# Nine of eleven row pairs of an FFN's last projection as block products, with every second weight's low parts on GpSimd

## The chip, the cores and the metric

The kernel runs on one core of a Trainium2 chip. The metric is the device time of one execution in microseconds (us), and the kernel before has a median of 843.04 us over three runs (843.0 to 843.1). A core has engines that run side by side, each with its own queue of instructions: TensorE (PE, with its weight loads shown as PEld), VectorE (DVE), ScalarE (ACT), GpSimd (POOL) and SyncE (SP). In this kernel SP issues most of the DMA transfers, and POOL issues a few that add while they copy.

## The reference, cut to what matters

One residual block on 512 tokens of width 1024, all in float32: a mixing part (attention over chunks, and a gated recurrence), and then a SwiGLU feed-forward network, which is what this case is about.

```python
hn = rmsnorm(h, norm_ffn_g[l])
gu = hn @ w_ffn_in[l]                  # 1024 x 5632
g, up = jnp.split(gu, 2, axis=-1)      # 512 x 2816 each
h = h + (jax.nn.silu(g) * up) @ w_ffn_out[l]   # 2816 x 1024
return rmsnorm(h, final_norm_g)
```

The last projection multiplies the activations (512 x 2816) by `w_ffn_out` (2816 x 1024). With tiles of 128, the 2816 rows of the weight are 22 row tiles, or 11 pairs of them.

## The kernel before, in words

**Float32 out of two parts.** TensorE works here on a reduced float32 format. Each operand is split into a high part, which ACT makes by a copy, and a low part, the rest, which DVE makes by a subtraction (`split`, lines 84 to 87). A product is then three matmuls (`mm3`, lines 78 to 82: lines 80, 81 and 82 of the profile): high by high, high by low, low by high. The first reads only high parts; the second is the first to read the weight's low part.

**Block products.** A row pair with its two row tiles, and the tokens and output columns in halves, is a 2 x 2 by 2 x 2 product of blocks. Done plainly it takes eight block products, 48 matmuls of 512 columns. It can be had from seven block products, 42 matmuls, if sums and differences of blocks are multiplied instead. The kernel does three pairs plainly (`plain`, pairs 0 to 2) and eight as block products (`paired`, pairs 3 to 10; `N_PLAIN` on line 34).

For a paired row pair the weight side needs the blocks of the left output half as they are (`fo0`), one block with its sum (`t3b`), and sums of blocks (`t12` and `t4`). These sums are made in DRAM, long before: during the attention SP copies blocks (`out_copy`, `COPIES`), and later POOL issues transfers that add to them (`out_add`, `ADDS_AT`, `ADDS`), one transfer for each group of `GROUP` row pairs. The activation side needs for each pair a left tile (`a_first`), a right tile with four additions on DVE (`a_sums`, lines 1518 to 1526), then a second form of the left tile (`a_second`), and a last part of the right tile (`a_last`). Each ends in a `split`, so in an ACT copy and a DVE subtraction.

**The order of the last projection.** It is written out by hand for PE, DVE and ACT (`manual_schedule`), so these three do their instructions in the order of the code. SP and POOL are put in order by a planner. The stages are:

1. the plain pairs on the left output half (24 matmuls each). After each but the first, left and right tiles are made for the paired ones;
2. P: for each pair two products with `fo0` (`p_one`, `p_two`; 12 matmuls). The second products of the last three pairs are held back to the end. `p_then` spreads the left tiles and some of the right tiles between them;
3. the plain pairs but the last two on the right output half (one pair here, 24 matmuls);
4. T: two products for each pair with `t12` (`t_one`, `t_two`), again with three held back. The remaining right tiles are made one per step, ahead of the weights of that step, and from the fifth pair on the second form of a left tile behind each step;
5. U: two products for each pair with `t3b`. All but the last six pairs come first, with all their first products ahead of their second ones, and then the last six in the same way;
6. the products with `t4`, then the last two plain pairs, the additions to `h`, the norm and the output.

**Weights.** `weights(name, ahead)` makes sure that a weight and `ahead` more after it are on their way, in one fixed list (`fo0`, the right half of the plain pairs but two, `t12`, `t3b`, `t4`, the last two plain ones). Making one means a tile to hold its two parts (seven in turn), a raw tile to load it to (five in turn, free again when the low part is made), the loads on SP, the high part on ACT, and the low part. For `t12`, `t3b` and `t4` the low part is put off (`high_first`, `lows`): it enters DVE's order when the next weight is made (`low_parts`), and so behind whatever the code has put there meanwhile. In T's last step `weights` is asked for `t3b` of the second pair, and only after the left tiles that remain for all the others.

The running sums of the products live in PSUM banks; when a sum is complete DVE adds it to `h` (`h_add`, line 1546; `h_sum`, line 1551). Those additions wait for PE, and what is written behind them on DVE waits too.

Of the kernel before, what the change touches and what calls it, by code (L numbers as in the profile page):

```python
# [9 lines left out]
F32R = mybir.dt.float32r  # L10
# [4 lines left out]
P = 128  # L15
# [15 lines left out]
V_CW, V_CB, V_BR, V_BI, V_LAM, V_BM, V_GF = 0, 32, 40, 48, 56, 64, 80  # L31
NV = 88
CW = 256
N_PLAIN = 3
GROUP = 2
COPIES = [1] * 16
ADDS_AT = (9, 11, 13, 15)
ADDS = {"fg1": 1, "fg2": 1}
PAIR_TILES = 2 * (11 - N_PLAIN) - (4 - (N_PLAIN - 1))


@with_exitstack
def block_kernel(ctx: ExitStack, tc: tile.TileContext, x, norm_mix_g, w_in, b_merge, rel_table,
# [3 lines left out]
    pe, dve, act, pool, sp = nc.tensor, nc.vector, nc.scalar, nc.gpsimd, nc.sync  # L47

    def pool_of(name, bufs=1, side="left"):
        return tc.tile_pool(name=name, bufs=bufs, side=side, reuse_waits="tile")  # L50
# [21 lines left out]
    def f(ap):  # L72
        return ap.bitcast(F32)
# [62 lines left out]

    plain, paired = list(range(N_PLAIN)), list(range(N_PLAIN, FT // 2))

# [44 lines left out]
    def out_raw_home(name):  # L183
        n = raw_count[0] = raw_count[0] + (out_room[0] is not None)
        pl, bufs = (out_room[0], 2) if n % 5 in (2, 4) else (wp, 3)
        return pl.tile([P, 2, S], F32, tag="raw", bufs=bufs, name=f"raw_{name}")

    def out_home(name):
        n = out_count[0] = out_count[0] + 1
        pl, bufs = (wp, 4) if n % 7 in (1, 2, 3, 4) else (out_room[0], 3)  # L190
        return pl.tile([P, 2, 2, S], F32R, tag="whl", bufs=bufs, name=f"whl_{name}")

    lows = []

    def high_first(hi, lo, src):

        act.activation(hi, src, AF.Copy)
        lows.append(lambda: dve.tensor_sub(lo, src, f(hi)))

    def low_parts(n=0):  # L200

        while len(lows) > n:
            lows.pop(0)()

    t4_raw = {}
    groups = [paired[n:n + GROUP] for n in range(0, len(paired), GROUP)]
    out_t = {}
# [6 lines left out]
    def out_t_at(kind, i):  # L214
        t, n = out_t[kind, i]
        return t[:, n]
# [21 lines left out]
    def step(todo, n=1, **more):  # L238

        for _ in range(min(n, len(todo))):  # L240
            what, *of = todo.pop(0)
            what(*of, **more)

    def out_sums(name, rows):

        kind, i = name.split("_")
        i = int(i)
        if kind == "t4":

            hl = spare[0].tile([P, 2, S], F32R, tag="act", bufs=13, name=f"whl_{name}")  # L250
        else:
            hl = out_home(name)

        if kind == "t4":
            if i not in t4_raw:
                raw = out_raw_home(name)
                for n, i_ in enumerate(paired[i - paired[0]:][:2]):
                    sp.dma_start(out=raw[:, n], in_=out_t_at("t4", i_))
                    t4_raw[i_] = raw[:, n]
            raw = t4_raw[i]  # L260
        else:
            raw = out_raw_home(name)
        if kind == "t12":
            sp.dma_start(out=raw[:, 0], in_=out_t_at("t1", i))
            sp.dma_start(out=raw[:, 1], in_=out_t_at("t2", i))
        elif kind == "t3b":
            sp.dma_start(out=raw[:, 0], in_=out_t_at("t3", i))
            sp.dma_start(out=raw[:, 1], in_=w_ffn_out[rows + P:rows + 2 * P, S:])
        else:
            low_parts()  # L270
            high_first(hl[:, 0], hl[:, 1], raw)
            return lambda part, k, at=every: hl[:, part, at]
        low_parts()
        high_first(hl[:, 0], hl[:, 1], raw[:])
        return lambda part, k, at=every: hl[:, part, k, at]

    v_t1, v_t2 = [], []
# [143 lines left out]
    def prefetch(n):  # L421
        while len(made) < min(n, len(chunks), index.get(barrier[0], len(chunks))):
            name, parts, rows, kts = chunks[len(made)]
            if name[:2] == "v_":
                made.append(v_weights(name[2:]))
                continue
            if name[:2] == "o_" or name[:3] == f_units[0]:
                made.append(kept_weights(name[0], name.split("_")[1]))
                continue
            if name[:3] in f_units:  # L430
                made.append(f_weights(*name.split("_")))
                continue
            if not parts:
                made.append(out_sums(name, rows))
                continue
            tiles = []
            wide = sum(width for *_, width in parts)
            step = 4 * CW // wide
            for k in range(0, kts, step):
                n_ = min(step, kts - k)  # L440
                if name in extra:
                    hl = extra[name].tile([P, 2, n_, wide], F32R, tag="whl", bufs=4, name=f"whl_{name}_{k}")
                elif name[:2] == "fo":
                    hl = out_home(name)
                else:
                    hl = wp.tile([P, 2, n_, wide], F32R, tag="whl", bufs=4, name=f"whl_{name}_{k}")
                if (name, k) not in raws:
                    load(name, k)
                raw = raws.pop((name, k))
                low_parts()  # L450
                split(hl[:, 0], hl[:, 1], raw[:])
                tiles.append(hl)
            made.append(lambda part, k, at, tiles=tiles, step=step: tiles[k // step][:, part, k % step, at])

    def weights(name, ahead=1):
        prefetch(index[name] + 1 + ahead)
        if index[name] + 1 == len(made):
            low_parts()
        return made[index[name]]
# [511 lines left out]
    def x_sums():  # L971

        s, s3 = (zp.tile([P, 4, 256], F32, tag="late", bufs=2, name=f"v_s{n}")[:] for n in (1, 3))
        out = {}

        def parted(key, src):
            pl, tag = (aw, "v") if key == "s4" else (aw2, "pt")
            hi, lo = (pl.tile([P, 4, 256], F32R, tag=tag, bufs=4, name=f"v_{key}{n}") for n in "hl")
            split(hi[:], lo[:], src)
            out[key] = hi, lo  # L980

        def chain(dst, first_, *rest):
            (op, one, two) = first_
            tc.keep_in_program_order(op(dst, one, two))
            for op, one in rest:
                op(dst, dst, one)

        add, sub = dve.tensor_add, dve.tensor_sub
        chain(s, (add, x_block(1, 0, 0), x_block(1, 1, 0)), (add, x_block(1, 0, 1)), (add, x_block(1, 1, 1)))
        parted("s1", s)  # L990
        chain(s, (sub, s, x_block(0, 0, 0)), (sub, x_block(0, 0, 1)))
        parted("s2", s)
        chain(s3, (sub, x_block(0, 0, 0), x_block(1, 0, 0)), (add, x_block(0, 0, 1)), (sub, x_block(1, 0, 1)))
        chain(s, (sub, x_block(0, 1, 0), s), (add, x_block(0, 1, 1)))
        return out, parted, s, s3
# [159 lines left out]
    sums = x_sums()  # L1155
# [9 lines left out]
    with tc.manual_schedule(engines={mybir.EngineType.PE}):  # L1165
        v_all(sums)
        for h in range(HEADS):
# [4 lines left out]
            weigh(h, pp)  # L1172
            step(copies, COPIES[h])
            if h in ADDS_AT:
# [11 lines left out]
    for j in range(KT):  # L1186
# [11 lines left out]
        else:  # L1198
            i = j - 4
# [91 lines left out]
    acp = ctx.enter_context(pool_of("act", 13))  # L1291
# [160 lines left out]
    for unit in f_units[1:]:  # L1452
        n, last = int(unit[2]), unit == f_units[-1]
# [51 lines left out]
    left, right_ = {}, {}  # L1505
    spare_tags = ["t10", "t11", "t20", "t21"][N_PLAIN - 1:]
    ohp = []

    def pair_tile(i, name):
        if spare_tags:  # L1510
            return sums_room.tile([P, 2, 2, 256], F32R, tag=spare_tags.pop(), bufs=1, name=f"{name}{i}")
        return ohp[0].tile([P, 2, 2, 256], F32R, tag="act", bufs=PAIR_TILES, name=f"{name}{i}")

    def a_first(i):
# [42 lines left out]
    def h_scale(cc, t, at=every):  # L1557

        if t not in scaled:
            scaled[t] = ohp[0].tile([P, D], F32, tag="act", bufs=PAIR_TILES, name=f"hg{t}")  # L1560
        n = slice(cc * S + at.start, cc * S + at.stop)
# [24 lines left out]
    def spread(todo, n):  # L1586

        for _ in range(min(n, len(todo))):
            todo.pop(0)()

    with tc.manual_schedule(engines={mybir.EngineType.PE, mybir.EngineType.DVE, mybir.EngineType.Activation}):
# [3 lines left out]
        sums = [lambda i=i: a_sums(i) for i in paired]  # L1595
# [34 lines left out]
        pw = {}  # L1630

        def p_one(n, i):
            pw[i] = weights(f"fo0_{i}", 4 if n < 4 else 2)
            if n == 0:
                for t in (2, 3):
                    h_add(0, t, po[t][:])
            for a in range(2):
                out_block(pq[a][:], left[i], 0, a, pw[i], 0, n == 0)
            if i == paired[-1]:
                for a in range(2):  # L1640
                    h_add(0, a, pq[a][:])
# [4 lines left out]

        def p_then(n):
            spread(firsts, 1)
            if n in (1, 3, 5):
                spread(sums, 1)  # L1650

        two_sided(p_one, p_two, p_then)
        for a in range(2):
# [112 lines left out]
```

## Time and profile before

| | |
|---|---|
| median of three runs | 843.04 us |
| the profiled execution | 843.44 us |
| its span, first to last instruction | 841.7 us |
| PE busy | 833.2 us, 99% |
| DVE, ACT, POOL busy | 662.8, 516.7, 160.5 us |
| granted TensorE clock | 0.999 |
| first matmul of the last projection, last one | 726.62, 835.48 us |

Rows of the timeline give the start, the length, the engine, the line of the kernel, the operation, and the tiles (written <- read) with their shapes. "x2" means two instructions of one kind behind each other, whose length is then that of both. Brackets tell how long the engine had been idle before, and what ended it. Instructions that follow each other on DVE overlap a little, so what one costs in a queue is the distance from its start to the next one's.

### The profile page before, as it was taken

The page shows a single profiled execution, that of the slowest core. Times are in us where ns is not written, and L with a number is a line of the kernel's source. Part 1 is how long each engine was busy: PE and PEld are TensorE (multiplying, and loading weights), DVE is VectorE, ACT ScalarE, POOL GpSimd, SP SyncE. Part 2 cuts the span into 40 slices and gives each one's busy share as a digit, 9 for nine tenths or more (in the row PEclk, how much of TensorE's full clock was granted, in tenths as well). Part 3 has the DMA queues.
Part 4 walks back from the last instruction along what each step waited for, and adds up shares of the span by engine and source line. Part 5 has one row for each costly group of instructions (what it writes and reads, how often), then busy time and mean ns, then how long its engine had stood idle before and what let it go on. Part 6 is the DMA issues. An engine that isn't in the chain of part 4 may idle for free.

```text
span 841.7 us, 11921 instructions
## 1 busy us (share of the span) xinstructions
PE 833.2 (99%) x4230; PEld 706.8 (84%) x4230; DVE 662.8 (79%) x974; ACT 516.7 (61%) x850; POOL 160.5 (19%) x219
## 2 busy tenths in 40 slices
PE   8999999999999999999999999999999999999997
PEld 6988888888888888888888888888888999988886
DVE  6688778887959888887568767888777878997784
ACT  7686858774356688878544547663764465455543
POOL 3502030221020043433211012005102321300000
PEclk9999999999999999999999999999999999999999
DMA  8466487553645455538558875555955576644442
GB/s 291 165 228 225 147 300 254 184 206 104 197 156 150 138 149 139 175 129 216 101 136 220 325 280 172 156 176 170 236 170 155 150 189 185 213 154 149 156 171 100
DMA packets 107323, 153.98 MB, mean 183 GB/s; under 512 B 8216, under 2 KB 66160, under 8 KB 106752
## 3 DMA queue, kind: packets, MB, share of 16 engines
q1 hardware_dynamic: 102304, 141.32, 51.6%
q0 software_dynamic: 3728, 8.96, 6.4%
q10 hardware_dynamic: 1232, 2.95, 0.9%
q8 instruction: 33, 0.54, 0.2%
q14 instruction: 26, 0.21, 0.1%
HBM read 139.53 MB, written 30.45 MB: 202 GB/s over the span
## 4 chain that ended last, share of the span: by engine, by line
PE 96%; DMA 2%; DVE 1%; ACT 1%; issue 0%; ACTq 0%; SPq 0%; DVEq 0%
PE fu_x L81 2%; PE fu_x L80 2%; PE fu_x L82 2%; PE o L1134 2%; PE fg_x L80 2%; PE fg_x L82 2%; PE fg_x L81 2%; PE pT L1114 2%; PE s L1085 2%; PE po_xr L80 2%; PE po_xr L81 2%; PE po_gb L80 2%; PE po_ga L80 2%; PE po_gr L82 2%; PE po_xr L82 2%; PE po_gr L80 2%
## 5 line engine op out<-in xcount | busy, mean ns | idle before, releaser
L1098 ACT ACTIVATE p<-p,m 128x384 f32<-128x384 f32 (+2 forms) x64 | 35.8, 559 | 14.9 <-DVE m L1097 14.4
L1103 POOL TENSOR_SCALAR p<-p,rl 128x128 f32<-128x128 f32 (+3 forms) x61 | 37.3, 628 | 14.7 <-DVE rl L1099 13.3
L1355 POOL TENSOR_TENSOR sg<-sg,keep_fu_x 128x512 f32<-128x512 f32 x8 | 14.5, 1817 | 100.3 <-DVE keep_fu_x L1354 100.3
L87 DVE TENSOR_TENSOR pp<-pT,pp 128x384 fp32r<-128x384 f32 (+1 forms) x48 | 27.0, 598 | 4.4 <-ACT pp L86 3.3
L87 DVE TENSOR_TENSOR whl_fu_w<-raw_fu_w,whl_fu_w 128x1024 fp32r<-128x1024 f32 (+1 forms) x18 | 23.3, 1300 | 8.8 <-ACT whl_fu_w L86 8.8
L87 DVE TENSOR_TENSOR whl_fu_t<-t_fu,whl_fu_t 128x1024 fp32r<-128x1024 f32 (+1 forms) x18 | 24.7, 1384 | 5.0 <-ACT whl_fu_t L86 4.9
L745 POOL MEMSET bias<- 64x64 f32 x16 | 2.4, 152 | 136.9 <-DMA bias<-ext_d 107.6
L81 PE MATMUL po_xr<-xnT,whl_xr 128*128 128x512 f32 (+1 forms) x80 | 27.7, 353 | 0.0
L81 PE MATMUL po_gr<-xnT,whl_gr 128*128 128x512 f32 (+1 forms) x80 | 27.5, 347 | 0.0
L82 PE MATMUL po_gr<-xnT,whl_gr 128*128 128x512 f32 (+1 forms) x80 | 27.3, 347 | 0.0
L82 PE MATMUL po_xr<-xnT,whl_xr 128*128 128x512 f32 (+1 forms) x80 | 27.2, 347 | 0.0
L80 PE MATMUL po_gr<-xnT,whl_gr 128*128 128x512 f32 (+1 forms) x80 | 27.2, 347 | 0.0
L80 PE MATMUL po_xr<-xnT,whl_xr 128*128 128x512 f32 (+1 forms) x80 | 26.3, 351 | 0.4 <-ACT xnT L656 0.4
L1097 DVE CUSTOM_DVE_ANT_0 p<-s,bias 128x384 f32<-128x384 f32 (+2 forms) x48 | 25.4, 552 | 1.4
L86 ACT ACTIVATE whl_fu_w<-raw_fu_w 128x1024 fp32r<-128x1024 f32 (+1 forms) x18 | 17.7, 987 | 13.6 <-issue 7.6
L80 PE MATMUL po_k<-xnT,whl_qk 128*128 128x512 f32 x64 | 25.5, 399 | 0.0
L80 PE MATMUL po_q<-xnT,whl_qk 128*128 128x512 f32 x64 | 25.5, 399 | 0.0
L80 PE MATMUL po_ga<-xnT,whl_ga 128*128 128x512 f32 x64 | 25.4, 398 | 0.0
L80 PE MATMUL po_gb<-xnT,whl_gb 128*128 128x512 f32 x64 | 25.3, 395 | 0.0
L82 PE MATMUL po_q<-xnT,whl_qk 128*128 128x512 f32 x64 | 25.0, 390 | 0.0
L82 PE MATMUL po_k<-xnT,whl_qk 128*128 128x512 f32 x64 | 25.0, 390 | 0.0
L82 PE MATMUL po_ga<-xnT,whl_ga 128*128 128x512 f32 x64 | 25.0, 390 | 0.0
(691 smaller groups left out, 3074.0 us busy)
## 6 DMA issues: line engine op xcount, KB each, us to landing
raw_qk<-in_w_in_dram SPq DMA_DIRECT2D x32, 256.0 KB, 3.2
out_t<-in_w_ffn_out_dram SPq DMA_DIRECT2D x16, 512.0 KB, 5.5
raw_fu_w<-in_w_ffn_in_dram SPq DMA_DIRECT2D x16, 512.0 KB, 4.4
raw_fo<-in_w_ffn_out_dram SPq DMA_DIRECT2D x14, 512.0 KB, 4.4
raw_t<-out_t SPq DMA_DIRECT2D x24, 256.0 KB, 3.3
raw_xr<-in_w_in_dram SPq DMA_DIRECT2D x8, 512.0 KB, 5.6
raw_gr<-in_w_in_dram SPq DMA_DIRECT2D x8, 512.0 KB, 4.2
raw_ga<-in_w_in_dram SPq DMA_DIRECT2D x8, 512.0 KB, 4.6
```

What stands on the lines that cost most here:

```text
L80: pe.matmul(o, sh, mh, start=start, stop=False, skip_group_check=parts)
L81: pe.matmul(o, sh, ml, start=False, stop=False, skip_group_check=parts)
L82: pe.matmul(o, sl, mh, start=False, stop=stop, skip_group_check=parts)
L86: act.activation(hi, src, AF.Copy)
L87: dve.tensor_sub(lo, src, f(hi))
L1085: pe.matmul(sc, qs, kk[:, part, e, 0:w], start=part == 0, stop=part == 1, skip_group_check=qb < 2)
L1097: dve.tensor_tensor_reduce(prob[qb][:], src, prob[0][:] if qb == 0 else bias[:, S - w:S], -1.0, 3e38, ALU.add, ALU.min, nmax[:, qb:qb + 1])
L1098: act.activation(prob[qb][:], prob[qb][:], AF.Exp, bias=nmax[:, qb:qb + 1], scale=-1.0, accum_out=lsum[:, qb:qb + 1])
L1103: eng.tensor_scalar(prob[qb][:], prob[qb][:], rl[:, qb:qb + 1], 1.0, ALU.mult, ALU.mult)
L1114: pe.transpose(pt[:, at * P:(at + 1) * P], prob[qb][:, kb * P:(kb + 1) * P], ident[:])
L1134: pe.matmul(po[:, S - n:S], st, pp[i][:, part, lo:lo + n], start=kb == 0 and part == 0, stop=kb == NT - 1 and part == 1)
L1355: (pool if keep and (unit != f_units[-1] or side) else dve).tensor_mul(o, o, keep_ if keep else bank)
```

## The change

Pair 2 goes from the plain ones to the paired ones, so that pairs 0 and 1 are plain and 2 to 10 are block products. No plain pair is left for stage 3. In U the first group holds three pairs instead of two. The DRAM sums are made in three groups of three pairs instead of four of two: twelve copies (one in each of heads 0 to 11) and twelve additions. Three right tiles are still made in T; the two before them (pairs 6 and 7) are made when P's last first product has been issued. The last step of P asks for one weight more ahead. One of the tiles for a pair is taken from the pool of the activations. And for `t12` and `t3b` of every second paired pair (3, 5, 7 and 9) the low part is a GpSimd subtraction, which is not put off.

```diff
-N_PLAIN = 3
-GROUP = 2
-COPIES = [1] * 16
+N_PLAIN = 2
+GROUP = 3
+COPIES = [1] * 12 + [0] * 4
...
-PAIR_TILES = 2 * (11 - N_PLAIN) - (4 - (N_PLAIN - 1))
+PAIR_TILES = 2 * (11 - N_PLAIN) - (4 - (N_PLAIN - 1)) - 1
...
-    def high_first(hi, lo, src):
+    def high_first(hi, lo, src, own=False):
 
         act.activation(hi, src, AF.Copy)
-        lows.append(lambda: dve.tensor_sub(lo, src, f(hi)))
+        if own:
+            pool.tensor_sub(lo, src, f(hi))
+        else:
+            lows.append(lambda: dve.tensor_sub(lo, src, f(hi)))
...
-        high_first(hl[:, 0], hl[:, 1], raw[:])
+        high_first(hl[:, 0], hl[:, 1], raw[:], (i - paired[0]) % 2 == 1)
...
+    pair_spare = [True]
...
+        if pair_spare and pair_spare.pop():
+            return acp.tile([P, 2, 2, 256], F32R, tag="act", bufs=13, name=f"{name}{i}")
...
-            pw[i] = weights(f"fo0_{i}", 4 if n < 4 else 2)
+            pw[i] = weights(f"fo0_{i}", 4 if n < 4 else 2 + (i == paired[-1]))
...
-            if n in (1, 3, 5):
-                spread(sums, 1)
+            if n in (1, 3, 5) or n == len(paired) - 1:
+                spread(sums, 1 + (n > 5))
```

## The prediction

> **What bounds the kernel now.** I read the page's head first, then cut the last projection into its stages with a table of windows.
>
> ```profile
> span 841.7 us, 11921 instructions
> ...
> PE 833.2 (99%) x4230; PEld 706.8 (84%) x4230; DVE 662.8 (79%) x974; ACT 516.7 (61%) x850; POOL 160.5 (19%) x219
> ```
>
> ```profile
> 726.62:742.97 16.35, 16.35 (x74) 13.53 (x73) 14.97 (x22) 10.25 (x15) 2.44 (x1) 1.00 0.67 215
> 742.97:764.73 21.76, 21.76 (x97) 18.03 (x96) 17.22 (x29) 8.14 (x11) 0.00 (x0) 1.00 0.37 121
> 764.73:770.17 5.44, 5.44 (x25) 4.50 (x24) 5.37 (x10) 4.88 (x9) 0.00 (x0) 1.00 0.27 96
> 770.17:791.93 21.76, 21.76 (x97) 18.03 (x96) 17.39 (x25) 14.09 (x20) 0.00 (x0) 1.00 0.54 180
> 791.93:813.69 21.76, 21.76 (x97) 18.02 (x96) 21.76 (x37) 12.03 (x21) 0.63 (x1) 1.00 0.66 231
> 813.69:835.60 21.91, 21.91 (x109) 18.59 (x107) 11.10 (x22) 6.87 (x17) 0.00 (x0) 1.00 0.09 33
> ```
>
> The columns are the stretch, its length, then busy time and count of PE, PEld, DVE, ACT and POOL, granted clock, DMA share and GB/s. The stretches are: three plain pairs on the left output half (72 matmuls); the P stage of eight block pairs (96); the plain pair 0 on the right half (24); the T stage, with the t12 weights (96); the U stage, with t3b (96); t4 and the last plain pieces. PE is full in every one, at granted clock 1.00: 96 matmuls in 21.76 us are 0.2267 each, 24 are 5.44, a block product (6 matmuls) is 1.36. So time is won only by fewer matmuls and lost only by making PE wait. The engine closest to making it wait is DVE: 17.2 to 21.76 us in stages of 21.76. Its rows:
>
> ```profile
> 753.10 0.42 DVE L1522 TENSOR_TENSOR s<-act 128x256 f32<-128x256 f32 x1
> ...
> 755.30 0.42 DVE L1522 TENSOR_TENSOR s<-act 128x256 f32<-128x256 f32 x1
> ```
>
> ```profile
> 760.17 1.37 DVE L1546 TENSOR_TENSOR h<-p_out,h 128x512 f32<-128x512 f32 x2 [1.12 <-PE p_out L82]
> 764.25 1.37 DVE L1551 TENSOR_TENSOR h<-po_out,h 128x512 f32<-128x512 f32 x2 [2.71 <-PE po_out L82]
> ...
> 781.92 1.22 DVE L198 TENSOR_TENSOR whl_t<-raw_t,whl_t 128x1024 fp32r<-128x1024 f32 x1
> 787.37 1.37 DVE L1546 TENSOR_TENSOR h<-h,p_out 128x512 f32<-128x512 f32 x2 [4.23 <-PE p_out L82]
> 788.65 2.36 DVE L198 TENSOR_TENSOR whl_t3b<-raw_t3b,whl_t3b 128x1024 fp32r<-128x1024 f32 x2
> 790.93 0.68 DVE L87 TENSOR_TENSOR left<-act,left 128x512 fp32r<-128x512 f32 x1
> 791.53 1.29 DVE L1546 TENSOR_TENSOR h<-q_out,h 128x512 f32<-128x512 f32 x2
> 792.74 2.49 DVE L87 TENSOR_TENSOR left<-act,left 128x512 fp32r<-128x512 f32 x4
> 795.14 6.95 DVE L198 TENSOR_TENSOR whl_t3b<-raw_t3b,whl_t3b 128x1024 fp32r<-128x1024 f32 x6
> ```
>
> From these, queued start to start: a weight's low part 1.14 (2.36 less 1.22), a left tile 0.60 (2.49 less 0.68, by three), one pair's sums with the right tile's low part 2.20 (755.30 less 753.10), two bank additions 1.28 (788.65 less 787.37). DVE's spare time is the bracketed waits for PE, 4.23 us at the end of T the largest.
>
> **The change part by part.**
>
> *Matmuls.* A plain pair costs 48, a block pair 7 x 6 = 42. 3 x 48 + 8 x 42 = 480 become 2 x 48 + 9 x 42 = 474: 6 x 0.2267 = **1.36 us less**. This is all that can be won here; the code from t4 on hangs on PE as before.
>
> *Fewer, larger copies and sums in DRAM.* 16 transfers of 512 KB on SP's queue and 16 on POOL's become 12 of 768 KB on each.
>
> ```profile
> out_t<-in_w_ffn_out_dram SPq DMA_DIRECT2D x16, 512.0 KB, 5.5
> ...
> out_t<-in_w_ffn_out_dram POOLq DMA_DIRECT2D x8, 512.0 KB, 6.6
> out_t<-out_t POOLq DMA_DIRECT2D x8, 512.0 KB, 6.0
> ```
>
> ```profile
> SPq L744 <- DVE m L1097: 59.3, 13, 7.5
> ```
>
> I cost them at nothing. On SP they go past the bias and q/k loads of heads 0 to 11, where SP waits 59.3 us for free bias tiles anyway; without that cover one copy would hold the next load back by half its landing, 2.7 us. On POOL nothing else queues behind the four fewer sums but small cell copies.
>
> *Plain and P stages.* PE now reaches P one plain pair sooner, at 742.97 - 5.44 = 737.53, with left tiles 2 and 3 and right tile 2 made. After its two bank additions (end about 738.7) DVE makes left 4 to 10 (7 x 0.60), sums 3 to 5 (3 x 2.20) and low parts of fo0_7 to 10 (4 x 1.14): 15.4, to 754.1. The last first product of P starts at 737.53 + 6 x 2.72 + 2 x 1.36 = 756.57, so 2.4 us are spare: nothing. The GpSimd low part of a plain act tile that goes is off the path.
>
> *The low parts on GpSimd.* Odd block pairs' t12 and t3b low parts, 8 in all. The same shape stands in the trace, with what DVE did beside it:
>
> ```profile
> 690.72 2.42 POOL L1444 TENSOR_TENSOR act_lo<-act,act_hi 128x1024 fp32r<-128x1024 f32 x1 [11.15 <-ACT act_hi L1443]
> 701.50 2.40 POOL L1444 TENSOR_TENSOR act_lo<-act,act_hi 128x1024 fp32r<-128x1024 f32 x1 [8.36 <-ACT act_hi L1443]
> ...
> 728.26 2.44 POOL L1444 TENSOR_TENSOR act_lo<-act,act_hi 128x1024 fp32r<-128x1024 f32 x1 [7.26 <-ACT act_hi L1443]
> ```
>
> ```profile
> 690.82 0.69 DVE L1347 TENSOR_TENSOR act<-fg_y,keep_fg_x 128x512 f32<-128x512 f32 x1 [0.45 <-PE fg_y L82]
> ...
> 701.83 3.75 DVE L87 TENSOR_TENSOR whl_fu_t<-t_fu,whl_fu_t 128x768 fp32r<-128x768 f32 x2 [1.24 <-ACT whl_fu_t L86]
> 705.51 1.84 DVE L87 TENSOR_TENSOR whl_fu_w<-raw_fu_w,whl_fu_w 128x768 fp32r<-128x768 f32 x2
> ...
> 729.17 3.74 DVE L87 TENSOR_TENSOR whl_fo<-raw_fo,whl_fo 128x1024 fp32r<-128x1024 f32 x2 [0.75 <-ACT whl_fo L86]
> ```
>
> Two DVE low parts of 768 take 1.84 alone and 3.75 when GpSimd's started 0.33 before them; two of 1024 take 2.36 alone and 3.74 beside the one of 728.26, ending at 732.91. GpSimd ends there at 730.70; one queued low part (1.14) and one whole (1.22) after it make 733.06. So DVE stood still until GpSimd was done, less about 0.14. The row at 690.82, whose first input is a PSUM bank, is not stretched. Each moved low part therefore saves DVE 1.14 and, where DVE has SBUF work queued, stops it for 2.40 - 0.14 = 2.26. Bounds: 0 (it falls on a wait or on bank additions) and 2.26.
>
> The Trainium skill, page "SBUF — State Buffer", section "Who interferes with whom", says that a DVE instruction with two SBUF inputs and a GpSimd instruction reading SBUF block each other fully, for the whole instruction. Taken literally a stop is 2.40, an estimate that makes the sum below some 0.6 us longer; the 0.14 of the rows decides.
>
> *T stage.* Two of the sums now come at P's end, none is saved. The last first product of P starts at 756.57; DVE's bank addition follows a start by 0.88 (before: 742.97 + 5 x 2.72 + 2 x 1.36 = 759.29, and the row 760.17), so at 757.45. From there, in DVE's written order up to the low part of t12_10: two additions 1.28, sums 6 to 10 11.0, two additions 1.28, low parts of t12_4, 6, 8, 10 4.56, left tiles (second form) 2 to 5 2.40: 20.5, to 778.0. PE needs t12_10's low part in the second matmul of its product: T starts at 737.53 + 9 x 2.72 = 762.01, plus 6 x 2.72 + 2 x 1.36 + 0.23 = 781.28. Without stops DVE is 3.3 early. But GpSimd's t12_5, 7 and 9 fall inside this chain, where only sums, low parts and left tiles are queued: 3 x 2.26 = 6.8, to 784.8. **PE waits 3.5 us**, in pieces from t12_4 to t12_10. Bounds 0 and 3.9 (2.40 each).
>
> *U stage.* Of nine pairs the first group is now three: t3b_4 is wanted third, ahead of all second products, but only t3b_2 and t3b_3 are made before the left tiles. Count from the release R of t12_10: PE has 5 matmuls, the held products (4.08), two t3b products (2.72) and one matmul, so it wants t3b_4's low part at 1.13 + 4.08 + 2.72 + 0.23 = 8.2. DVE: bank additions from 0.65 to 1.9, t3b_2's low part to 3.1, left 6 to 3.7, a wait for the second banks (1.13 + 4.08 - 0.68 + 0.2 = 4.7), additions to 6.0, left 7 to 10 to 8.4, t3b_4's low part done at 9.6. Late by 1.4 without any stop. The stops: t3b_7's raw tile comes free with t3b_2's low part at 3.1,
>
> ```profile
> L267 SPq DMA_DIRECT2D raw_t3b<-out_t x8: 319/319/320, 772.4 to 796.4; - x8
> ...
> L197 ACT ACTIVATE whl_t3b<-raw_t3b x8: 1041/1055/1068, 780.6 to 799.8; 128x1024 fp32r<-128x1024 f32 x8
> ...
> DMA to landing us min/median/max: 2.6/3.2/4.0
> ```
>
> its two loads land some 3.5 later (3.2 and the first issue's 0.32), ACT's high part takes 1.05: GpSimd starts at about 7.7, just before t3b_4's turn, and the 2.26 lands on the path. t3b_5's falls near 3.2 to 5.6, on left 6 and the 1.0 of waiting: 0 to 1.3. Late 3.7 to 5.0, taken 4.3 as the middle. Bounds 1.4 (no stop) and 5.2. What is late next: t3b_6 and 8 follow at 1.14 while PE still owes three second products (4.08), and t4 comes 16 us later, so nothing more.
>
> *Sum.* Against the profiled execution's span: 841.7 - 1.36 + 3.5 + 4.3 = 848.1 (843.44 us of its own time, 1.7 around it, becomes 849.9). The median shown is 0.4 lower: 843.04 + 6.4 = **849.5 us**.
>
> **Rivals.**
> A. *The stall cools PE's clock.* One wait near 4 to 5 us stands in U.
>
> ```profile
> 1.18 5.27 PE L478 MATMUL busy<-idle 128*128 128x512 bf16 x16 [1.18 <-DVE eps_t L484]
> ...
> 835.48 0.28 PE L82 MATMUL po_last<-whl_fo,act_lo 128*128 128x256 f32 x1
> ```
>
> ```profile
> 840.00:840.50 0.50, 0.00 (x0) 0.00 (x0) 0.00 (x0) 0.00 (x0) 0.00 (x0) 1.00 0.12 37
> 840.50:841.00 0.50, 0.00 (x0) 0.00 (x0) 0.00 (x0) 0.00 (x0) 0.00 (x0) 0.81 0.00 0
> ```
>
> The first 16 matmuls take 5.27, 1.6 above 16 x 0.2267. At the end the clock is granted in full until after 840.5, 4.7 us behind the last matmul. Against: the wait is likely shorter than that. Price 1.6: 851.1. The Trainium skill, "TensorE: Matmul & The Clock Gate", section "What's actually happening", says that the clock halves after one idle window of about 3.4 us, free-running; by that it would happen in perhaps a third of such waits. The 4.7 seen here is compatible.
>
> B. *Only one of the two waits comes*: stops in T fall on DVE's waits, or t3b_7 lands later than t3b_4's turn. 843.04 - 1.36 + about 4.3 = 846.0, or with T alone and U at 1.4, 846.6. Against: T's chain has no wait once it starts.
>
> C. *The other side: GpSimd and DVE run side by side.* Place: the t12 and t3b low parts; price 0 per stop. Then T is on time, U is late by 1.4 and the six matmuls pay for it: 843.04 - 1.36 + 1.4 = 843.1. It decides from stops below about 0.5 us each. For it: only the three overlaps quoted speak, all on other tiles. Against: all three stretched.
>
> D. *Everything is hidden*, t3b_4 too (its tile made earlier than I read): 843.04 - 1.36 = 841.7, 0.16% less.
>
> **How the numbers follow.** Forecast 0.64, A 0.12, B 0.12, C 0.07, D 0.05. The forecast with A and B spans from 846.0; the unknowns add upward 0.4 in T, 0.9 in U and A's 1.6, to some 852.5. The range is 845.8 to 852.5 and leaves out C, D and a little above. A measurement of this kernel tells about 0.2% (1.7 us) from no change. Slower: forecast, A, B, 0.88 less a little for doubt in the order I read: 0.86. C and D lie within 0.2%: 0.12. Faster by more would need over 1.7 where 1.36 is on offer: 0.02.
>
> **What would show it.** Matmuls of the last projection down by 6; PE with idle time for the first time there, on t12 products and then, largest, at the third t3b product, both put down to DVE low parts; DVE's left, s and whl_t rows stretched to 1.5 to 3 us wherever GpSimd's 2.4 us rows stand; no wait in P. It is wrong if those DVE rows keep 0.42, 0.68 and 1.22 beside GpSimd, or if PE stays full from the first plain pair to the last piece.

## The result: 1.4% slower, by 5.5 us more than predicted

The changed kernel takes 854.98 us, the median of six runs (851.69 to 860.05), where the kernel before, run beside it, takes 843.02 (842.85 to 843.17). The ratio is 1.0143, with a 95% interval of 1.0125 to 1.0162. The direction was right, the time was not: 849.5 was predicted, and 852.5 was the end of the range. Three disturbed executions among all those reported here, of 1039, 1195 and 2983 us, are left out of every median and range.

The head of the page of the changed kernel, whose profiled execution took 855.65 us:

```profile
span 853.9 us, 11922 instructions
...
PE 837.1 (98%) x4224; PEld 707.1 (83%) x4224; DVE 667.9 (78%) x975; ACT 517.4 (61%) x855; POOL 179.1 (21%) x218
```

The six matmuls are gone (4224 for 4230), and yet TensorE is busy for 3.9 us more. So some of its matmuls run longer. The last projection in a table of windows, P from 739.77, the T stage from 764.25 and U from 794.62:

```profile
739.77:764.25 24.48, 24.48 (x109) 20.28 (x108) 22.87 (x40) 12.46 (x19) 2.76 (x1) 1.00 0.48 150
764.25:794.62 30.37, 27.41 (x109) 21.03 (x108) 25.03 (x33) 19.00 (x28) 14.77 (x5) 0.94 0.49 156
794.62:820.00 25.38, 21.84 (x89) 17.59 (x88) 20.08 (x30) 12.65 (x23) 5.77 (x3) 0.93 0.63 199
```

P is full at full clock, as foretold. T and U have idle TensorE time, and their granted clock is 0.94 and 0.93 instead of 1.00. P also begins late: one plain pair sooner than before was to be 737.53, and it is 739.77. The next list is what TensorE waited for from 300 us on (us in all, times, the longest):

```profile
PE p_out L81 <- DVE whl_t3b L201: 3.5, 1, 3.5
PE p_out L81 <- DVE whl_t L201: 2.2, 2, 1.8
PE fu_x L81 <- DVE whl_fu_w L87: 1.0, 1, 1.0
PE p_out L81 <- POOL whl_t L199: 0.6, 1, 0.6
PE fg_x L81 <- DVE whl_fg_t L87: 0.3, 1, 0.3
PE pT L1117 <- POOL p L1106: 0.3, 1, 0.3
```

The kernel before has none of these. Three are of the last projection, and three lie in the attention (`pT`) and the FFN's first part (`fg_x`, `fu_x`), where the change touches little but the DRAM transfers.

The account of the 12.2 us between the spans: matmuls -1.4; P late by 739.77 - 737.53 = 2.2; T's waits 4.1 and U's wait 3.8 (matmul starts further apart than the usual 0.2267, which takes in the fractions beside the waits listed); two stretches at half clock, 1.6 each (eight matmuls each, 0.427 from start to start and not 0.2267). The sum is 11.9.

The half clock is seen best in windows cut at the instants where the granted clock changes. Columns as before: PE's busy time is the third number, the granted clock the third from the end.

```profile
785.52:788.93 3.41, 1.58 (x8) 1.06 (x7) 2.58 (x4) 3.41 (x6) 2.39 (x1) 1.00 0.49 153
788.93:792.34 3.41, 3.41 (x10) 2.65 (x9) 2.60 (x4) 2.67 (x4) 2.24 (x2) 0.50 0.76 265
792.34:795.76 3.42, 3.42 (x17) 2.81 (x16) 1.62 (x3) 0.53 (x2) 1.47 (x1) 1.00 0.80 225
795.76:799.17 3.41, 1.97 (x9) 1.31 (x7) 3.41 (x4) 1.89 (x2) 2.39 (x1) 1.00 0.33 113
799.17:802.58 3.41, 1.31 (x6) 1.10 (x7) 3.41 (x4) 0.00 (x0) 0.36 (x1) 1.00 0.50 158
802.58:806.00 3.42, 3.42 (x10) 2.66 (x9) 0.90 (x1) 0.74 (x1) 0.00 (x0) 0.50 0.93 285
```

Two windows at 0.50 show 10 matmuls each where a full one shows 17. One is preceded by T's wait for `t12_10`, the other by U's wait for `t3b_4`.

The stops of DVE are there too. Two of its rows in T, where one sum took 0.42 before and four left tiles 2.49:

```profile
770.36 2.62 DVE L1528 TENSOR_TENSOR s<-act 128x256 f32<-128x256 f32 x1
...
783.04 3.42 DVE L87 TENSOR_TENSOR left<-act,left 128x512 fp32r<-128x512 f32 x4 [1.19 <-ACT left L86]
```

Its rows about U's wait, with the one of GpSimd that lies beside them:

```profile
794.14 1.37 DVE L1552 TENSOR_TENSOR h<-q_out,h 128x512 f32<-128x512 f32 x2 [2.59 <-PE q_out L82]
795.43 4.64 DVE L87 TENSOR_TENSOR left<-act,left 128x512 fp32r<-128x512 f32 x4
800.00 3.48 DVE L201 TENSOR_TENSOR whl_t3b<-raw_t3b,whl_t3b 128x1024 fp32r<-128x1024 f32 x3
```

```profile
796.78 2.75 POOL L199 TENSOR_TENSOR whl_t3b<-raw_t3b,whl_t3b 128x1024 fp32r<-128x1024 f32 x1 [2.97 <-ACT whl_t3b L197]
```

Four left tiles that took 2.49 before take 4.64 beside `t3b_7`'s low part on GpSimd, and `t3b_4`'s low part, next in line, ends at 801.22. TensorE had waited 3.54 for it.

### The profile page after: what moved, and what is told of

Read it like the earlier page. It is cut to its first block, busy times and chain, and to the rows that moved or that the text cites. A ratio compares the mean times of both kernels' runs of the same rounds, so it can differ in the third digit from the quotient of the medians.

```text
span 853.9 us, 11922 instructions
## 1 busy us (share of the span) xinstructions
PE 837.1 (98%) x4224; PEld 707.1 (83%) x4224; DVE 667.9 (78%) x975; ACT 517.4 (61%) x855; POOL 179.1 (21%) x218
## 4 chain that ended last, share of the span: by engine, by line
PE 91%; DVE 5%; DMA 2%; ACT 1%; issue 1%; POOL 0%; SPq 0%; ACTq 0%; DVEq 0%
PE fu_x L81 2%; PE fu_x L82 2%; PE fu_x L80 2%; PE o L1137 2%; PE pT L1117 2%; PE s L1088 2%; PE po_xr L81 2%; PE po_xr L80 2%; PE po_gb L80 2%; PE fg_x L81 2%; PE fg_x L82 2%; PE po_ga L80 2%; PE po_gr L82 2%; PE po_gr L81 2%; PE po_gr L80 2%; PE po_xr L82 2%
## 5 line engine op out<-in xcount | busy, mean ns | idle before, releaser
L86 ACT ACTIVATE whl_fu_t<-t_fu 128x1024 fp32r<-128x1024 f32 (+1 forms) x18 | 17.5, 986 | 13.7 <-PE fu_x L82 9.2
L80 PE MATMUL po_ga<-xnT,whl_ga 128*128 128x512 f32 x64 | 25.4, 397 | 0.0
```

Of the source, the lines that this page charges most:

```text
L80: pe.matmul(o, sh, mh, start=start, stop=False, skip_group_check=parts)
```

## The experiments

Theory after the result: (a) GpSimd's low parts stop DVE, as predicted; (b) the larger transfers of the DRAM sums hold up the loads of the attention and the FFN's first part; (c) a wait of some 2 us, much shorter than the prediction allowed, halves the clock for 3.4 us. The rivals differ from run to run and stand with the expectations. Each ratio is to the kernel before, run beside the variant.

### All low parts on VectorE

```diff
-        high_first(hl[:, 0], hl[:, 1], raw[:], (i - paired[0]) % 2 == 1)
+        high_first(hl[:, 0], hl[:, 1], raw[:])
```

> The changed kernel with all t12 and t3b low parts back on DVE; nothing else differs. My theory (GpSimd's low parts stop DVE): without stops T's chain ends in time but for about 0.2 us at t12_4, U's third t3b product waits about 1.6, the wait in the FFN's first part (2.0) stays, PE's clock stays up: 843.0 - 1.4 + 0.2 + 1.6 + 2.0 = 845.4 us (844.5 to 847.2). Rival (DVE is overloaded, GpSimd relieves it): eight low parts more, 9 us, on DVE, so more than the changed kernel's 855.

849.26 us (846.02 to 850.77), ratio 1.0062 (1.0041 to 1.0083). Against the changed kernel that is 5.7 us less, but 4 us more are left than expected. Its waits from 300 us on, in the execution of 850.77:

```profile
PE fg_x L81 <- DVE whl_fg_t L87: 2.5, 1, 2.5
PE p_out L81 <- DVE whl_t3b L201: 1.4, 1, 1.4
PE o_z L82 <- DVE ms L87: 1.3, 1, 1.3
PE p_out L81 <- DVE whl_t L201: 0.3, 1, 0.3
PE pT L1117 <- POOL p L1106: 0.3, 1, 0.3
```

In the last projection the figures come out: U's wait was worked out at 1.4 without stops (1.6 in the expectation, with the low parts that DVE now makes itself) and is 1.4, and T's is 0.3. From its first product of P to the end this execution takes 105.4 us, the changed kernel's 114.1, so there GpSimd's low parts cost 8.7 us, with the half clock behind their waits. The rest lies far ahead, in the attention (`pT`), the product behind it (`o_z`) and the FFN (`fg_x`, with a stretch of half clock behind it): P begins at 743.56, 6.0 late.

### The odd low parts on GpSimd, alone

The kernel before, with only the `own` form of `high_first` and its use for every second paired pair.

> The kernel before with one part of the change, the low parts of every second t12 and t3b on GpSimd. My theory: four stops each in T and U; T has spare time and takes them, U does not: waits of about 4.4 at t3b_5, 0.2 to 0.4 at t3b_3 and t3b_10, and one stretch of half clock behind the long one (1.6): 843.0 + 4.9 + 1.6 = 849.5 us (847 to 851). Rival (GpSimd works beside DVE): DVE has 9 us less to do and the time stays 843.0.

846.82 us (846.4 to 847.41), ratio 1.0046 (1.0029 to 1.0063): 3.8 us, below my range. With eight pairs, U's first group has two weights, and the lateness comes in four small waits (1.6 us in three for `whl_t3b`, 0.9 the longest, and 0.6 for a bank addition; by matmul starts they come to 3.5); no clock falls. The rival, no cost, is out.

### The larger groups, alone

```diff
-GROUP = 2
-COPIES = [1] * 16
+GROUP = 3
+COPIES = [1] * 12 + [0] * 4
```

> The kernel before with groups of three row pairs in the DRAM sums (12 copies and 12 additions, 768 KB for a full group), nothing else. My theory: the larger additions in the FFN's first unit hold up the loads beside them, and PE waits there as in the changed kernel: 843.0 + 1.5 to 2.0 = 844.5 to 845.0 us, all of it before 640 us of the span. Rival (the waits there come from the plan of the whole kernel, which differs in the changed one): 843.0.

849.00 us (846.14 to 852.11, four runs), ratio 1.007 (1.0043 to 1.0096), above the 844.5 to 845.0 of the theory. This is the term that I had put at nothing: alone, and with eight pairs, it costs 3 to 9 us. No usable profile of it exists, so this run shows the sum and not the place.

### The waits filled with matmuls of no use

The changed kernel, with nine matmuls ahead of `t12_10`'s product and fifteen ahead of `t3b_4`'s, into a bank that is written anew later; they add nothing to the output.

```diff
+        def filled(n):
+            for _ in range(n):
+                pe.matmul(po[3][:], actT[0][0][:, 0:P], actT[0][0], start=True, stop=True)
...
+            if i == paired[-1]:
+                filled(9)
...
+                if i == paired[2]:
+                    filled(15)
```

> The changed kernel with matmuls of no use in PE's two longest waits: 9 ahead of the product with t12_10 and 15 ahead of the first one with t3b_4 (into a bank that is written anew later). My theory (waits of some 2 us and more halve PE's clock): the waits stay, the two stretches of half clock behind them go, 3.2 us: 855.0 - 3.2 = 851.8 us, as the one run of the changed kernel at clock 1.000 (851.7); granted clock 0.998 or more. Rival (the clock drops for another cause, or the added matmuls cost what they take): 855 or, with all 24 of them on top, 860.

853.47 us (851.21 to 857.33), ratio 1.0127 (1.0098 to 1.0157). In the profiled execution no window of T or U is at half clock, which agrees with (c). As a saving it is inconclusive: 851.8 was expected, and the interval overlaps that of the changed kernel. TensorE waited 1.6 us in the attention there, where it had 0.3 in the changed kernel's profile, and not at all in the FFN: with the same transfers, the place of the loss differs from execution to execution.

### Transfers of 512 KB again, all else as changed

```diff
-GROUP = 3
-COPIES = [1] * 12 + [0] * 4
+GROUP = 2
+COPIES = [2] * 4 + [1] * 12
...
-ADDS = {"fg1": 1, "fg2": 1}
+ADDS = {"fg1": 1, "fu1": 1, "fg2": 1}
```

> The changed kernel whole, but its copies and additions in DRAM in groups of two rows as before: 20 copies and 20 additions of 512 KB in place of 12 and 12 of 768 KB (four steps of the attention issue two copies each, and the FFN's second unit issues four additions more). If the size of a single transfer is what held up the loads ahead of the last projection, 2 to 5 us of the 12 go and the time is 851 (849.5 to 852.5), with P's first product at or before 738. If the bytes moved are the cause, or the delay has nothing to do with these transfers, 854 to 856 as the changed kernel.

851.51 us (848.68 to 853.78), ratio 1.0087 (1.0064 to 1.0111), 3.5 us below the changed kernel. From 300 us on the waits are now those of the last projection alone, with the same figures as in the changed kernel:

```profile
PE p_out L81 <- DVE whl_t3b L201: 3.5, 1, 3.5
PE p_out L81 <- DVE whl_t L201: 2.2, 2, 1.8
PE p_out L81 <- POOL whl_t L199: 0.6, 1, 0.6
```

P begins at 737.54, which is the 737.53 of the prediction, and from there to the end it takes 114.0 us, as the changed kernel does. The six runs fall into two heaps: 848.68, 849.47 and 849.52 at a mean clock of 0.998, and 853.50, 853.74 and 853.78 at 0.994 or 0.995. One window at half clock takes 0.5 x 3.41 / 852 = 0.002 off the mean, so the second heap fits two of them. The profiled execution, 853.50, has two, one behind each of the two waits. The faster heap lies at the 849.5 of the prediction. Two windows make 3.2 of the 4.5 us between the heaps; where the other 1.3 come from is open, since no run of the faster heap was profiled.

### The ninth pair without GpSimd and without large transfers

As the run before, with all low parts on VectorE and U's groups split two and seven, so that `t3b_4` is no longer wanted ahead of the second products.

```diff
-        for some in (pairs_[:-6], pairs_[-6:]):
+        for some in (pairs_[:2], pairs_[2:]):
...
-            if some is not pairs_ and len(some) == 6:
+            if some is not pairs_ and len(some) == 7:
```

> Nine pairs with 512 KB transfers, all low parts by VectorE, and the third projection's two groups split two and seven, so that the weight waited for in the second group is no longer the third of the first: of the change only the ninth pair and the sums moved ahead are left. If GpSimd's low parts and the size of the transfers are the whole of the loss, six matmuls are saved (1.4 us) and a wait of at most 0.5 us is left: 842.0 (841.5 to 843.0). If the ninth pair's added bytes and DVE's added work cost time by themselves: 844 to 849.

843.87 us (842.15 to 849.36, twelve runs), ratio 1.0006 (0.9992 to 1.0021): no difference from the kernel before, and between the two forecasts. U's wait is gone. What is left from 300 us on takes back what the six matmuls save:

```profile
PE fg_x L82 <- DVE whl_fg_w L87: 0.9, 1, 0.9
PE p_out L81 <- DVE whl_t L201: 0.4, 1, 0.4
```

### The copies large, the additions as before; and the other way round

The kernel before with one DRAM tile per kind, so that copies and additions can be grouped apart.

```diff
-    groups = [paired[n:n + GROUP] for n in range(0, len(paired), GROUP)]
+    by_copy = [paired[n:n + GROUP_COPY] for n in range(0, len(paired), GROUP_COPY)]
+    by_add = [paired[n:n + GROUP_ADD] for n in range(0, len(paired), GROUP_ADD)]
```

With `GROUP_COPY, GROUP_ADD` at 3, 2:

> The kernel before, eight pairs, with its 16 copies of 512 KB joined into 12 of up to 768 KB and its 16 additions as they were. If the additions are what delays the loads, nothing: 843.1 (842.9 to 843.6). If the copies, issued in the order of SP's queue among the loads, are the cause: 846 to 850, as with both.

843.53 us (843.05 to 845.06), ratio 1.0001 (0.9992 to 1.0009). With 2, 3:

> The kernel before, eight pairs, with its 16 copies of 512 KB as they were and its 16 additions joined into 12 of up to 768 KB. If the additions are the cause: 846 to 850, as with both, with waits of TensorE where the FFN's raw_fg_w and raw_fu_w land 7 us or more after their issue. If the copies are: 843.1 (842.9 to 843.6).

847.45 us (847.18 to 850.21), ratio 1.0052 (1.0037 to 1.0066). So it is the additions, and the copies cost nothing, as predicted. The place was not the one that I named: in the profiled execution no wait stands in the FFN, and the only one from 300 us on is in the attention. The wait, whose largest piece ends at 389.28, and the windows about it:

```profile
PE pT L1118 <- POOL p L1107: 2.8, 3, 2.2
```

```profile
388.40:391.81 3.41, 1.83 (x11) 1.26 (x12) 1.88 (x3) 1.85 (x6) 3.29 (x6) 1.00 1.07 387
391.81:395.22 3.41, 3.41 (x11) 2.67 (x10) 2.81 (x6) 2.75 (x7) 0.44 (x1) 0.50 0.92 311
```

What `p` waited for is on GpSimd's own queue, the corner of a bias tile that is cleared once its load has landed. First this kernel's row, then that of the kernel before:

```profile
387.66 0.15 POOL L749 MEMSET bias<- 64x64 f32 x1 [9.73 <-DMA bias<-ext_d]
```

```profile
385.13 0.15 POOL L745 MEMSET bias<- 64x64 f32 x1 [7.03 <-DMA bias<-ext_d]
```

The addition was issued on GpSimd's queue at 376.55 (before: 376.97) and landed at 386.05 (before: 383.61). The bias load was issued at 379.15 (before: 379.25), and its corner was cleared 1.6 us behind the addition's landing in this kernel and 1.5 us behind it before. So the load is done soon after the addition, and the larger addition landed 2.4 us later. The packets show why: from 379.5 to 382.0 in the kernel before, and to 382.5 in this one, the 16 DMA engines move packets of GpSimd's queue (q0, the addition) alone. From 382 to 384 the kernel before is at SP's (q1, with the bias load), and this one still at the addition's (packets, MB, share of the engines); first this kernel, then before:

```profile
q0 software_dynamic: 149, 0.28, 85.3%
q1 hardware_dynamic: 66, 0.14, 26.1%
```

```profile
q1 hardware_dynamic: 230, 0.45, 80.2%
q0 software_dynamic: 31, 0.03, 9.5%
```

In the changed kernel the same is seen in the FFN, where additions and loads of `raw_fg_w` were issued between 590 and 612; first the changed kernel, then before (KB each, median us to landing):

```profile
out_t<-out_t POOLq DMA_DIRECT2D x3, 768.0 KB, 8.8
raw_fg_w<-in_w_ffn_in_dram SPq DMA_DIRECT2D x2, 512.0 KB, 8.2
```

```profile
out_t<-out_t POOLq DMA_DIRECT2D x3, 512.0 KB, 7.4
raw_fg_w<-in_w_ffn_in_dram SPq DMA_DIRECT2D x2, 512.0 KB, 4.5
```

In the changed kernel DVE waits for the second of these loads until 606.84, and its rows behind it stay late: the low part of a `whl_fg_w` comes at 612.58 (before: 608.06) and that of the `whl_fu_w` that TensorE waits for at 627.01 (before: 623.16). TensorE's wait for it, 1.0, ends at 628.28.

### Each large addition as three small ones

As the run with large additions, each issued as three of 256 KB behind each other.

```diff
+        for g in ([i] for i in g):
```

> The run with the larger additions alone, with each addition of 768 KB issued as three of 256 KB one behind the other at the same step: the bytes in flight at each step are the same, the single transfers are smaller. If the bytes in flight at once are what holds up the loads of the attention and the FFN, it stays at 846 to 849. If the length of a single transfer does it (a load issued behind it waits for the whole of it), the loss goes: 843.1 to 844.

848.53 us (848.03 to 850.16), ratio 1.0066 (1.0053 to 1.0079), with the same wait at the same place; the last of the three landed at 387.49. So it isn't the length of one transfer. That leaves what is in flight at a step, of the two that were set against each other.

### Waits of chosen lengths

The kernel before with a transpose of no use, which waits for a chain of ScalarE copies, in each of five units of the FFN's first part; its output is read by nothing.

```diff
+    def idle(unit, bank, cell):
+        act.activation(cell, bank[:, 0:P], AF.Copy)
+        for _ in range(IDLE[unit]):
+            act.activation(cell, cell, AF.Copy)
+        pe.transpose(mm_tile(f"idle_{unit}", "s")[:, 0:P], cell, ident[:])
...
         product(fz, unit, "t1", True)
+        idle(unit, fz[1], x2[0][:, 0:P])
```

> The kernel before with a transpose of no use in each of the last five units of the FFN's first part, which TensorE reaches behind the t1 product and which waits for 1, 2, 4, 6 and 9 ScalarE copies of 128x128 in a row, begun when that product is done: five waits of about 0.6, 1.0, 1.7, 2.4 and 3.5 us (estimates from ScalarE copies of about 0.3 us), 20 us or more apart. If a wait of about 2 us is enough to halve the clock for 3.4 us some 1.3 us behind it, the two longest, and perhaps the third, show matmuls at 0.43 us behind them, each costing 1.6 us more, and the others none: 843.0 + 9.2 + 3.2 to 4.8 = 855.4 to 857. If the clock falls only after 4.7 us, as the prediction had it, all matmuls behind the waits keep the 0.21 to 0.23 us pitch: 852.2.

One run, 865.68 us, above both forecasts, since the waits were longer than meant. The first was 0.43; the rows of the others (in brackets TensorE's idle time ahead):

```profile
598.03 0.33 PE L1458 MATMUL idle_fg<-ident,keep_fg_x 128*128 128x128 f32 x1 [2.54 <-ACT keep_fg_x L1457]
642.30 0.48 PE L1458 MATMUL idle_fu<-ident,keep_fu_x 128*128 128x128 f32 x1 [3.17 <-ACT keep_fu_x L1457]
685.53 0.45 PE L1458 MATMUL idle_fg<-ident,keep_fg_x 128*128 128x128 f32 x1 [3.48 <-ACT keep_fg_x L1457]
724.75 0.48 PE L1458 MATMUL idle_fu<-ident,keep_fu_x 128*128 128x128 f32 x1 [4.46 <-ACT keep_fu_x L1457]
```

The three longest were followed by half clock, the wait of 2.54 was not. Both theories as I had put them fail on that: 4.7 us is not needed, and 2 us is not always enough. The windows, again cut at the clock's changes and, about the wait of 2.54, carried back from them in steps of 3.413:

```profile
593.43:596.85 3.42, 2.06 (x10) 1.36 (x8) 1.53 (x2) 2.33 (x5) 0.19 (x1) 1.00 0.72 275
596.85:600.26 3.41, 2.23 (x15) 2.01 (x16) 2.45 (x3) 2.22 (x4) 0.83 (x1) 1.00 0.75 201
...
637.80:641.22 3.42, 1.33 (x6) 0.75 (x5) 1.22 (x1) 3.11 (x5) 0.00 (x0) 1.00 0.00 0
641.22:644.63 3.41, 2.33 (x6) 1.93 (x7) 3.23 (x3) 0.96 (x4) 0.00 (x0) 0.50 0.75 211
644.63:648.05 3.42, 3.42 (x9) 2.64 (x8) 2.63 (x3) 0.06 (x1) 0.00 (x0) 0.50 0.25 98
```

The wait of 2.54 is shared by two windows, 1.36 idle in one and 1.18 in the other, and neither is followed by half clock. The wait of 3.17 leaves 2.09 in one window, and the next is halved; that one has 1.08 idle itself, and the one after it is halved too.

### Two tries for a version that beats both

The nine pairs without GpSimd, as above, with the four further additions in the last unit of the FFN's first part in place of the third:

```diff
-ADDS = {"fg1": 1, "fu1": 1, "fg2": 1}
+ADDS = {"fg1": 1, "fg2": 1, "fu2": 1}
```

> The nine pairs with 512 KB transfers, all low parts by VectorE and the two-and-seven split, with the four additions more issued in the last unit of the FFN's first part in place of the third. If what is left of the loss is the loads that these four collide with (TensorE waited 0.9 us for a raw_fg_w weight behind them), it goes: 842.1 (841.6 to 842.8), just ahead of the kernel before. If the added copies in the attention or DVE's added work in the last projection hold it back, 843.5 to 844.5 as with the earlier place.

848.18 us (845.24 to 849.47, five runs), ratio 1.0052 (1.0038 to 1.0066): worse, and a miss. TensorE waits for `whl_fu_t` twice there, 1.4 us, and 1.8 in T. And with additions of 256 KB at 36 steps:

```diff
-GROUP = 2
+GROUP_COPY, GROUP_ADD = 2, 1
...
-ADDS_AT = (9, 11, 13, 15)
+ADDS_AT = range(4, 16)
```

> Nine pairs, all low parts by VectorE, the two-and-seven split, copies of 512 KB, and the additions in 36 transfers of 256 KB at 36 steps (twelve heads of the attention, all eight parts of its output projection, sixteen places of the FFN), so that fewer bytes are in flight at any step than in the kernel before. If bytes in flight at a step are what costs, nothing is left of it, the six matmuls saved count in full but for a wait of 0.4 us at the second projection's fifth product, and it is the fastest: 842.1 (841.7 to 842.6, before 843.3). If each further addition costs for itself (its place in POOL's queue, its issue of 1.1 us), 844 to 847.

846.45 us, ratio 1.0044 (1.0027 to 1.0061): a miss. The wait of the attention is down to 0.2, as the bytes in flight would have it, but a new one of 1.8 stands at the product behind it, `o_z`, with a half-clock window after it, and P begins at 741.91. Shortly ahead of the tile that `o_z` waited for, DVE stood 1.64 us for a load of `h` (0.73 in the kernel before), and an addition had been issued at 468.90, where the kernel before has none; that the one delayed the other fits and is not shown. No variant is faster than the kernel before.

## Why the prediction was wrong

*Two steps failed, and together they make 5.4 of the 5.5 us.* One is "Fewer, larger copies and sums in DRAM … I cost them at nothing". For the copies that holds: 0 (within 0.8 us). For the additions it doesn't: 4.4 us alone (3.1 to 5.6), 2.2 in the changed kernel's profiled execution, ahead of a P stage that starts late. The prediction looked at what queues behind the sums on GpSimd's queue, and found small cell copies; in the attention the clearing of the bias tiles and `p`, which TensorE waits for, stand there too. Above all it did not ask which loads go out while a sum is under way, though it had their landing times before it (6.6 and 6.0 us for 512 KB).

*The other is the clock, and it is the larger part.* The sum left it at full speed, and half clock stood in rival A alone, with a chance of 0.12 and one stretch. Rival A was right in kind, and its price, 1.6, is that of one stretch; there were two, 3.2 in all, and the first stands behind a T wait whose last piece is only 1.83 long. The prediction argued from the end of the kernel that TensorE must idle 4.7 us before the clock falls. The windows explain that row: the window in which the last matmul of the kernel before ended, 833.98 to 837.40, had 1.63 us idle and was not enough, and only the next, which was empty, was.

```profile
833.98:837.40 3.42, 1.78 (x15) 1.58 (x14) 3.24 (x11) 2.85 (x11) 0.00 (x0) 1.00 0.59 233
837.40:840.81 3.41, 0.00 (x0) 0.00 (x0) 0.48 (x1) 0.60 (x1) 0.00 (x0) 1.00 0.60 228
```

With both terms in their place the sum closes: 849.5 + 2.2 + 2 x 1.6 = 854.9, and 854.98 was measured. That it closes so well is partly luck: T came out 0.6 above its term and U 0.5 below, and the runs range from 851.69 to 860.05. The fastest run, 851.69 at a clock of 1.000, fits 849.5 + 2.2; it has no profile.

*Point by point, the rest held.* Matmuls: six fewer. P: full, and beginning at 737.54 once the transfers are small. GpSimd's stops: the DVE rows that were named are stretched (0.42 to 2.62 for a sum at 770.36, 2.49 to 4.64 for four left tiles), and the rows fed by PSUM keep 1.37 for two. T: 3.5 predicted, 4.1 measured, 0.2 above the upper bound, and not made up as worked out: the three stops are 2.2, 2.2 and 0.9, which is 1.5 less than three of 2.26, while DVE waited 1.4 in two places for high parts from ACT, and TensorE 0.6 for one of GpSimd's own low parts, neither of which was in the sum. U: 4.3 predicted as the middle of 3.7 to 5.0, 3.8 measured, since the stop of `t3b_5` fell on DVE's wait for PSUM banks; without stops 1.4 predicted and 1.4 measured. The place was right as well, the third weight of U's first group, and the two-and-seven split, which takes that demand away, takes the wait away. Rivals C and D, no cost and all hidden, are out by the run with GpSimd's low parts alone, and B by the waits list, where both waits stand.

## What to carry to other kernels

Where a transfer is made larger, list the loads that are issued while it is under way and when each is wanted, on all queues: the queue that it stands in is not the only one that waits. A price for a TensorE wait has two parts, its length and, from some 1.6 us on, a chance of 1.6 us more for a clock that is halved afterwards; two waits are two such chances, and they can make the times of one kernel fall into heaps. And where two engines share a row of work, cost the stop of the one for each instruction of the other: in the changed kernel that came within 0.6 us in both stages, and with eight pairs it was too high (4.9 for waits of 3.5).

## What the runs showed of the hardware

The clock goes by windows of fixed length that do not start with the wait. In the changed kernel the half clock begins at 788.93 and at 802.58, 13.65 apart, four times 3.413, and each lasts 3.41; in the run with chosen waits the changes fall on the same kind of grid through 80 us. A window is halved by what the one before it was: over the traces of this case, in the midst of matmul work, windows with up to 1.58 us idle were followed by full clock (1.36, 1.42 and 1.44 among them), and windows with 1.58, 1.68, 1.79, 1.83 and every longer idle time by half. In windows in which the kernel's last matmul ends, 1.63, 1.75 and 1.87 were still followed by full clock, and 1.95 by half. The bound lies between 1.58 and 1.87, then, about half of a window, and what else it depends on is open (the ends of matmuls are modelled, so a few hundredths are uncertain). So it depends on where a wait falls in the grid whether it costs its length or 1.6 more, and 2.54 us can go unpunished where 1.83 does not. The Trainium skill, "TensorE: Matmul & The Clock Gate", section "What's actually happening", has the free-running window of 3413 ns, and the trace agrees. It has the clock fall after at least one idle window; here the measurement differs, since a window less than half idle was enough (1.58 of 3.41). Windows that were themselves at half clock were followed by another at half with 1.08 and with 1.61 us idle, and by full clock with none or 0.20; where that bound lies, two cases do not tell.

The other thing not expected is that three additions of 256 KB issued together hold a load up as much as one of 768 KB. In the attention the traces show it: with small, large and divided additions alike, the DMA engines moved the additions' packets alone from 379.5 to 382.0, the bias load's issue being at 379.15 to 379.25, and the load was served as those ran out. So it waits for the bytes already in flight. That the same order is behind each of the other delays is argued from the landing times and not shown.
